# Moving one-hot matrices, weight splits and the last down product in a two-layer mixture-of-experts decoder on one core

## The chip, the cores and the metric

One core of a Trainium2 chip runs the whole program in one launch. The metric is device time in microseconds (us): the median over runs of the time of one execution. The program's engines are TensorE (PE in the profile, its weight loads PEld), VectorE (DVE), ScalarE (ACT), GpSimd (POOL) and SyncE (SP), which here issues nearly all the transfers.

## What is computed

Two layers over 256 tokens of width 1024. Each layer projects the tokens (w_in), runs three mixers (differential attention, a short gated convolution, cross attention into 256 memory tokens with its own weights w_mem_kv), merges them, adds the residual and normalises, and then does the same with a mixture of 16 experts (a gate, an up and a down matrix each), of which a token uses two, both in the one of four groups of experts that its router picks.

```
for l in range(2):
    mix = (sum_i sigmoid(G_i) * (y_i @ P_i)) @ w_out[l]
    x = layer_norm(ALPHA * x + mix, ln1_g[l], ln1_b[l])
    f = sum over the token's 2 experts e: gate_e * ((silu(x @ w_gate[l,e]) * (x @ w_up[l,e])) @ w_down[l,e])
    x = layer_norm(ALPHA * x + f, ln2_g[l], ln2_b[l])
```

## The kernel before

**Weights.** All large weights come in tiles of 1 MB, in one stream on SP's queue (`fetch`, L145), in the order of their use. A tile is asked for when its turn comes within a look-ahead (7 tiles in the mixers, 14 in the expert part, 8 near its end) and one of the 19 buffers it shares with the split weights is free. Weights of the mixers are split into a high and a low part, one half tile at a time (`pump`): ACT copies the high part (L179), DVE subtracts it to get the low part (L181). A product then takes three passes on PE: high weight by high and low activation (L217, L218), low weight by high activation (L220). Expert weights are used whole (`whole`), without a split.

**Order.** The order of PE's instructions is written out by hand: PE runs them in the order of the code. The orders of the other engines are set by a scheduler from the same code, so an edit moves rows there that it doesn't mention. Each engine runs its own list in order, and waits on semaphores.

**Start.** The first thing PE does is to transpose the memory tokens (`transposed`, L288: 16 transposes, four banks, each evicted as a high part on ACT, L206, and a low part on DVE, L207). Then come the first products with w_mem_kv: `mem_units` has four units of `ws_block`, which use halves 1 to 4, and then `mv_units` (L352), which use halves 5 to 8, first two passes with the high part of a half and then one with its low part.

**Expert part.** Eight steps p of two experts each. Each token has a slot in the list of its expert (at most 64 tokens an expert; a rare overflow is handled under an `If`, L1049, which every engine passes: it reads a count into a register and branches). For each group of four experts `places` (L885, DVE) builds a one-hot matrix pf, `gather` (L902, PE) multiplies the tokens by it and `scatter_maps` turns it (a copy pd on ACT, L912, small products on PE, L918 and L928) into the matrices that bring results back. These run one group ahead, in pieces between the projections (`steps`). A step then has the gate and up projections (`project`, L958), their product h (`gated`, L971, DVE), transposes of h (`hidden`, L980, with evictions L982 and L983), the `down` product (L993: 32 matmuls over four tiles of w_down, two tiles for each half of the inner dimension, both column halves for each), a split of its two column halves (yh on ACT, L206, yl on DVE, L207), and `combine` (L1007), which adds the results into four accumulators that stay in PSUM over all eight steps.

**End of a layer.** After the last `down` comes the `If`, then `combine` for the column halves, c = 0 and 1. `residual` adds the accumulators to x (L309, four times, on DVE) and gets the mean (L310), the variance (a square on ACT, L312) and its root (POOL, L313 and L314); `normalise` (L317, L321, DVE) applies gain and shift, loaded as gb by two transfers that POOL issues (L295, L296). In layer 0 the next layer's memory units follow on PE (their transposes are done earlier, at L288), beside the norm; then x is transposed.

Of the kernel before, what the change touches and what calls it, by code (L numbers as in the profile page):

```python
# [11 lines left out]
F32 = mybir.dt.float32  # L12
# [9 lines left out]
S = 256  # L22
DEPTH = 2
# [15 lines left out]
REV = (0, 0, 0, 1)  # L39
WARM = 20  # L40
WARM2 = 0
FILL = 20700
NU = 5
BETWEEN = 3
# [11 lines left out]
def trunk(ctx: ExitStack, tc: tile.TileContext, x, mem, positions, w_in, lq1, lk1, lq2, lk2, subln, conv_w,  # L56
# [9 lines left out]
    def bank(shape, tag="g", dtype=F32):  # L66
        return ps.tile(shape, dtype, name="ps_" + tag, tag=tag, bufs=4)
# [4 lines left out]
    def small(shape, dtype, name):  # L72
        return sb.tile(shape, dtype, name=name, tag="S", bufs=S_BUFS)
# [204 lines left out]
    cmask2 = cmask[:, None, :].to_broadcast([128, 2, 128])  # L278


    def transposed(src):

        th, tl = big([128, KD, S], F32R, "th"), big([128, KD, S], F32R, "tl")
        for k in range(0, KD, 2):
            b = bank([128, 2, S])
            for a in range(2):
                for t in range(2):
                    nc.tensor.transpose(b[:, a, t * 128:(t + 1) * 128],  # L288
                                        src[:, t, (k + a) * 128:(k + a + 1) * 128], ident)
            state["last"] = split(th[:, k:k + 2, :], tl[:, k:k + 2, :], b)  # L290
        return th, tl
# [8 lines left out]
        nc.gpsimd.tensor_scalar(v, v, EPS, None, op0=OP.add)  # L300
        nc.gpsimd.tensor_tensor(v, v, mhalf[:, 0:1], op=OP.pow)

    def residual(xt, acc, st, t):

        sm = sb.tile([128, 2], F32, name="rsum", bufs=2)
        nm, rstd = st[:, 0, t:t + 1], st[:, 1, t:t + 1]
        for c in range(2):
            v = xt[:, t, c * 512:(c + 1) * 512]
            nc.vector.scalar_tensor_tensor(v, v, ALPHA, acc[c], op0=OP.mult, op1=OP.add, accum_out=sm[:, c:c + 1])  # L309
        nc.vector.tensor_scalar(nm, sm[:, 0:1], sm[:, 1:2], -1.0 / D, op0=OP.add, op1=OP.mult)  # L310
        sq = small([128, D], BF, "sqx")
        nc.scalar.activation(sq, xt[:, t, :], AF.Square, bias=nm, accum_out=rstd)  # L312
        nc.gpsimd.tensor_scalar(rstd, rstd, 1.0 / D, EPS, op0=OP.mult, op1=OP.add)  # L313
        nc.gpsimd.tensor_tensor(rstd, rstd, mhalf[:, 0:1], op=OP.pow)  # L314
# [25 lines left out]
    def mv_units(act, dsts):  # L340
# [15 lines left out]
        for t in range(2):  # L356
            nc.scalar.activation(dsts[t], b[t], AF.Copy)

    mT = {0: transposed(mts.pop(0))}
    state["act"], state["dve"] = state["last"]  # L360
    units = mem_units(0)
# [498 lines left out]
    def warm(n):  # L860

        if n:
            b = bank([128, 4, 128])
            for _ in range(n):
                for i in range(4):
                    mm(b[:, i, :], identb, onesb, start=True, stop=True)

    def moe(l, xt, lt, st, gb):
        routing = route(l, lt, st)
        slot = next(routing)  # L870
# [10 lines left out]
        PF, XG, CT, GS = {}, {}, {}, {}  # L881

        def places(g):
            pf = small([128, 2, EG, CAP], F32R, "pf")
            ins = nc.vector.tensor_tensor(pf, i64[:, None, None, :].to_broadcast([128, 2, EG, CAP]),  # L885
                                          slot[:, :, g * EG:(g + 1) * EG, None].to_broadcast([128, 2, EG, CAP]),
                                          op=OP.is_equal)
            if g == 0:
                state["dve"] = ins
            PF[g] = pf  # L890

        def gather(g):

# [14 lines left out]

        def scatter_maps(g):

            pd = small([128, 2, 2, 2 * CAP], BF, "pd")
            nc.scalar.activation(pd, PF[g].bitcast(F32).rearrange("p t (i e) s -> p t i (e s)", i=2), AF.Copy)  # L912
            yield
            b = bank([128, 2, 2, 4])
            for i in range(2):
                for t in range(2):
# [13 lines left out]
            nc.scalar.activation(CT[g], b, AF.Copy)  # L930

        def group(g):
            places(g)
            yield from gather(g)
            yield from scatter_maps(g)
            yield

        state["ahead"] = STEADY
        prep = group(0)
        next(prep)  # L940
        gx, gp, cnti = next(routing)
# [34 lines left out]
        def hidden(h):  # L976

            b = bank([128, 4, 128])
            for f in range(4):
                nc.tensor.transpose(b[:, f, :], h[:, f, :], ident)  # L980
            hT = small([128, 4, 128], F32, "hT")
            nc.scalar.activation(hT[:, 0:2], b[:, 0:2], AF.Copy)  # L982
            nc.vector.tensor_copy(hT[:, 2:4], b[:, 2:4])  # L983
            return hT

        def down(h):
            bs = [bank([128, 512]) for _ in range(2)]
# [22 lines left out]
        def steps(n):  # L1010
            for _ in range(n):
                next(prep, None)
# [7 lines left out]
        for p in range(last + 1):  # L1020
# [19 lines left out]
            if pend is not None:  # L1040
                combine(*pend)
            steps(4)
            pend = p, down(hT[0])
            steps(4)
            if p < last:
                u = project(p + 1)
            else:
                most = nc.values_load(cnti[0:1, 0:1], min_val=0, max_val=S)
                with tc.If(most > CAP):  # L1049
                    overflow(l, xt, gx)  # L1050
        for c in range(2):
            combine(*pend, (c,))
        return xt, acc


    for l in range(DEPTH):
# [13 lines left out]
                state["act"] = scores(l, rT[1], lt, 1)  # L1070

        mixers(l, xT, done)
        xt, acc = moe(l, xt, lt, st, gb[0])
        last = l + 1 == DEPTH
        gb, st = gain_shift(ln2_g[l], ln2_b[l]), sb.tile([128, 2, 2], F32, name="lnst", bufs=2)
        for t in range(2):
            residual(xt, acc[t], st, t)
# [45 lines left out]
```

## Time and profile before

| what | value |
|---|---|
| time, median of 3 runs (least, most) | 1178.52 us (1176.53, 1179.73) |
| the profiled execution: its time, its span | 1174.73 us, 1173.0 us |
| PE busy | 1077.0 us, 92% of the span |
| DVE, ACT, POOL busy | 525.6, 421.2, 42.0 us |
| mean granted clock of TensorE | 0.970 |
| moved by DMA | 311.76 MB, mean 266 GB/s |

Times in the rows are in us from the span's start. Start and duration stand first in a row of a timeline; a stretch in brackets at its end is idle time of the engine before the row, and behind the arrow is what ended it. The profiled execution is 3.79 us faster than the median of the runs.

### The profile page before, as it was taken

The numbers are of one execution on the slowest core, as the hardware profiler recorded it, in microseconds if no ns is written. First come the engines' busy times: TensorE is split into PE (matmuls) and PEld (weight loads), VectorE is DVE, ScalarE is ACT, GpSimd is POOL, SyncE is SP. The second block draws the span as 40 slices with busy tenths as digits, with TensorE's granted clock in tenths as the row PEclk, the third lists the DMA queues.
The fourth block names the chain that finished last, engine by engine and source line by source line (L and its number), as shares of the span: only waits on it lengthen the run. The fifth ranks groups of instructions, "written<-read, shape, count | busy, mean of one in ns | idle before, by whom it ended". The sixth has DMA issues, their size and how long they took to land. (4 is left out here: it accounts for less than half of the span.)

```text
span 1173.0 us, 16717 instructions
## 1 busy us (share of the span) xinstructions
PE 1077.0 (92%) x6917; PEld 790.7 (67%) x6917; DVE 525.6 (45%) x874; ACT 421.2 (36%) x731; POOL 42.0 (4%) x87
## 2 busy tenths in 40 slices
PE   6988899999987999999989888999998889999995
PEld 6877899999974334343478878999998643344332
DVE  3968657545454111110447677565554611111114
ACT  3767645434332101010146666544433311011111
POOL 2000000000001000000010000000000110000001
PEclk9999899999988999999989899999999989999998
DMA  9925434555694999999996343356657669999993
GB/s 315 338 81 156 124 108 141 174 190 179 222 352 156 423 421 420 422 420 420 401 304 213 103 135 108 109 166 186 188 180 291 248 262 422 421 421 420 421 420 151
DMA packets 118609, 311.76 MB, mean 266 GB/s; under 512 B 5426, under 2 KB 83440, under 8 KB 93952
## 3 DMA queue, kind: packets, MB, share of 16 engines
q1 hardware_dynamic: 116192, 304.63, 70.0%
q0 software_dynamic: 1760, 5.35, 1.3%
q8 instruction: 56, 0.92, 0.3%
q10 hardware_dynamic: 576, 0.66, 0.2%
q14 instruction: 25, 0.20, 0.1%
HBM read 309.57 MB, written 1.05 MB: 265 GB/s over the span
## 5 line engine op out<-in xcount | busy, mean ns | idle before, releaser
L181 DVE TENSOR_TENSOR hl<-raw,hl 128x1024 fp32r<-128x1024 f32 x192 | 231.2, 1222 | 114.4 <-ACT hl L179 113.9
L217 PE MATMUL ps_g<-th,hl 128*128 128x256 f32 x960 | 246.6, 293 | 13.4 <-ACT hl L179 13.4
L179 ACT ACTIVATE hl<-raw 128x1024 fp32r<-128x1024 f32 x192 | 198.1, 1057 | 128.3 <-PE ps_g L220 64.9
L218 PE MATMUL ps_g<-tl,hl 128*128 128x256 f32 x960 | 242.1, 288 | 0.0
L958 PE MATMUL ps_g<-raw,xg 128*64 128x512 f32 x1024 | 229.1, 597 | 0.0
L217 PEld LDWEIGHTS ps_g<-th,hl 128*128 128x128 f32 x960 | 189.7, 198 | 18.1 <-ACT hl L179 15.9
L218 PEld LDWEIGHTS ps_g<-tl,hl 128*128 128x128 f32 x960 | 189.8, 198 | 0.1
L958 PEld LDWEIGHTS ps_g<-raw,xg 128*64 128x64 f32 x1024 | 71.5, 137 | 134.2 <-issue 131.5
L220 PE MATMUL ps_g<-th,hl 128*128 128x256 f32 x960 | 136.9, 286 | 0.7 <-DVE hl L181 0.7
L220 PEld LDWEIGHTS ps_g<-th,hl 128*128 128x128 f32 x960 | 125.8, 195 | 1.4 <-DVE hl L181 1.4
L993 PE MATMUL ps_g<-raw,hT 128*64 128x512 f32 x512 | 113.4, 595 | 0.0
L207 DVE TENSOR_TENSOR yl<-ps_g,yh 128x512 fp32r<-128x512 f32 x32 | 22.1, 690 | 149.8 <-ACT yh L206 149.8
L993 PEld LDWEIGHTS ps_g<-raw,hT 128*64 128x64 f32 x512 | 35.7, 137 | 68.0 <-issue 66.6
L206 ACT ACTIVATE yh<-ps_g 128x512 fp32r<-128x512 f32 x32 | 19.1, 597 | 116.9 <-PE ps_g L993 116.9
L971 DVE SCALAR_TENSOR_TENSOR h<-ps_g,gs,gate 128x512 f32<-128x512 f32 x16 | 17.8, 1111 | 89.3 <-PE ps_g L958 89.3
L352 PE MATMUL ps_g<-hl,th 128*128 128x512 f32 x192 | 52.9, 406 | 0.0
L982 ACT ACTIVATE hT<-ps_g 128x256 f32<-128x256 f32 x16 | 6.1, 383 | 116.7 <-PE ps_g L980 116.7
L678 PE MATMUL ps_acc<-hl,mh 128*128 128x512 f32 x128 | 37.7, 423 | 6.4 <-ACT hl L179 6.4
L902 PE MATMUL ps_g<-pf,xh 128*128 128x256 f32 x128 | 29.6, 316 | 13.2 <-DVE pf L885 13.2
L352 PEld LDWEIGHTS ps_g<-hl,th 128*128 128x128 f32 x192 | 36.0, 194 | 7.4 <-issue 0.7
L902 PEld LDWEIGHTS ps_g<-pf,xh 128*128 128x128 f32 x128 | 22.3, 212 | 25.3 <-issue 22.7
L907 ACT ACTIVATE xg<-ps_g 128x512 f32<-128x512 f32 x16 | 9.6, 597 | 76.7 <-PE ps_g L902 76.7
(236 smaller groups left out, 1276.0 us busy)
## 6 DMA issues: line engine op xcount, KB each, us to landing
raw<-in_w_in SPq DMA_DIRECT2D x64, 1024.0 KB, 5.7
raw<-in_w_exp_gate SPq DMA_DIRECT2D x64, 1024.0 KB, 14.5
raw<-in_w_exp_up SPq DMA_DIRECT2D x64, 1024.0 KB, 14.2
raw<-in_w_exp_down SPq DMA_DIRECT2D x64, 1024.0 KB, 17.0
raw<-in_w_mem_kv SPq DMA_DIRECT2D x8, 1024.0 KB, 12.4
raw<-in_w_br_attn SPq DMA_DIRECT2D x8, 1024.0 KB, 5.1
raw<-in_w_out SPq DMA_DIRECT2D x8, 1024.0 KB, 5.0
raw<-in_w_br_conv SPq DMA_DIRECT2D x8, 512.0 KB, 3.6
```

The source lines that it names most:

```text
L179: nc.scalar.activation(hi, src, AF.Copy)
L181: nc.vector.tensor_tensor(lo, src, hi.bitcast(F32), op=OP.subtract)
L206: return (nc.scalar.activation(hi, src, AF.Copy), nc.vector.tensor_tensor(lo, src, hi.bitcast(F32), op=OP.subtract))
L207: nc.vector.tensor_tensor(lo, src, hi.bitcast(F32), op=OP.subtract))
L217: mm(dst, wh[:, k0 + k, :], ah[:, k, :], start=(k == 0), stop=False)
L218: mm(dst, wh[:, k0 + k, :], al[:, k, :], start=False, stop=False)
L220: mm(dst, wl[:, k0 + k, :], ah[:, k, :], start=False, stop=(k == n - 1))
L352: mm(b[t], a[:, k, t * 128:(t + 1) * 128], ww[:, kk, :], start=(k == 0 and a is ah and ww is wh), stop=(k == KD - 1 and ww is wl))
L678: mm(acc[t][c], a[:, i, t * 128:(t + 1) * 128], ww[:, 0, c * 512:(c + 1) * 512], start=(j == 0 and s == 0), stop=(j == 3 and s == n - 1))
L902: mm(b[:, a], xs[:, t, (k + a) * 128:(k + a + 1) * 128], pf[:, t], start=(i == 0 and t == 0), stop=(i == 1 and t == 1))
L958: mm(b[both[i]], xg[:, k, c + i * CAP:c + (i + 1) * CAP], w[i][:, kk, :], start=(k == 0), stop=(k == KD - 1))
L993: mm(bs[c][both[i]], h[:, 2 * j + f, both[i]], w[i][:, f, c * 512:(c + 1) * 512], start=(j == 0 and f == 0), stop=(j == 1 and f == 1))
```

## The change

1. At the very start PE runs 56 matmuls of constant 128x128 bf16 matrices (`warm(WARM0)`, 14 times four) before the transposes of the memory tokens.
2. `places(g + 1)`, which builds pf of the next group, stands right behind the gather of group g, and makes pd too; `scatter_maps` no longer makes pd. For group 0 it stands ahead of everything.
3. The `If` of the overflow stands ahead of the last down product of a layer, no longer behind it. That product is done by column halves (`down_last`): all 4 tiles are taken at once, the column half 0 is finished over both halves of the inner dimension, then half 1 begins; ahead of the last quarter, half 0 is combined and added to x (`half`, `added`).
4. Except in the last layer, `pump(4)` splits four halves of the next layer's w_mem_kv between the last down product and the combine of column half 1. `residual` takes the sums of the half that was already added.

```diff
+WARM0 = 14
...
+    def added(xt, acc, sm, t, c):
+        v = xt[:, t, c * 512:(c + 1) * 512]
+        nc.vector.scalar_tensor_tensor(v, v, ALPHA, acc[c], op0=OP.mult, op1=OP.add, accum_out=sm[:, c:c + 1])
...
+    warm(WARM0)
     mT = {0: transposed(mts.pop(0))}
...
             PF[g] = pf
+            pd = PD[g] = small([128, 2, 2, 2 * CAP], BF, "pd")
+            nc.scalar.activation(pd, pf.bitcast(F32).rearrange("p t (i e) s -> p t i (e s)", i=2), AF.Copy)
...
         def group(g):
-            places(g)
             yield from gather(g)
+            yield
+            if g + 1 < E // EG:
+                places(g + 1)
             yield from scatter_maps(g)
             yield
...
+        def down_last(h, mid):
+
+            w = [(whole(), whole()) for _ in range(2)]
+            ys = []
+            for c in range(2):
+                b = bank([128, 512])
+                for j in range(2):
+                    if c and j:
+                        mid(ys[0])
+                    for f in range(2):
+                        for i in range(2):
+                            mm(b[both[i]], h[:, 2 * j + f, both[i]], w[j][i][:, f, c * 512:(c + 1) * 512],
+                               start=(j == 0 and f == 0), stop=(j == 1 and f == 1))
+                yh, yl = small([128, 512], F32R, "yh"), small([128, 512], F32R, "yl")
+                split(yh, yl, b)
+                ys.append((yh, yl))
+            return ys
...
             steps(4)
-            pend = p, down(hT[0])
-            steps(4)
             if p < last:
+                pend = p, down(hT[0])
+                steps(4)
                 u = project(p + 1)
-            else:
-                most = nc.values_load(cnti[0:1, 0:1], min_val=0, max_val=S)
-                with tc.If(most > CAP):
-                    overflow(l, xt, gx)
-        for c in range(2):
-            combine(*pend, (c,))
-        return xt, acc
+        most = nc.values_load(cnti[0:1, 0:1], min_val=0, max_val=S)
+        with tc.If(most > CAP):
+            overflow(l, xt, gx)
+        sums = [sb.tile([128, 2], F32, name="rsum", bufs=4) for _ in range(2)]
+
+        def half(y):
+            combine(last, [y], (0,))
+            for t in range(2):
+                added(xt, acc[t], sums[t], t, 0)
+
+        ys = down_last(hT[0], half)
+        if l + 1 < DEPTH:
+            pump(4)
+        combine(last, ys, (1,))
+        return xt, acc, sums
```

The lines of the changed kernel have moved: L885 is L891, L922 is L928, L971 is L980, L181 is L182, L207 is L208, L309 is L314, L310 is L323, L313 and L314 are L326 and L327, L317 and L321 are L330 and L334, L295 and L296 are L304 and L305, and the `If` is at L1075.

On DVE, in the expert part of layer 0, around the build of group 1's one-hot matrix. Before:

```order
288 L885 TENSOR_TENSOR pf<-i_106,slot 128x512
289 L905 COPY xg<-ps_g 128x512 x2
290 L922 TENSOR_REDUCE gs<-ps_g 64x2 x2
291 L971 SCALAR_TENSOR_TENSOR h<-ps_g,gs,gate 128x128x4
292 L885 TENSOR_TENSOR pf<-i_106,slot 128x512
293 L983 COPY hT<-ps_g 128x256
```

Now:

```order
288 L891 TENSOR_TENSOR pf<-i_106,slot 128x512
289 L913 COPY xg<-ps_g 128x512 x2
290 L891 TENSOR_TENSOR pf<-i_106,slot 128x512
291 L928 TENSOR_REDUCE gs<-ps_g 64x2 x2
292 L980 SCALAR_TENSOR_TENSOR h<-ps_g,gs,gate 128x128x4
293 L992 COPY hT<-ps_g 128x256
```

The second pf, which the gather of group 1 takes, stood behind the first h and now stands ahead of it.

On DVE, from the `If` at the end of layer 0 to the splits of w_mem_kv (hl). Before:

```order
351 L1049 UNCONDITIONAL_BRANCH
352 L309 SCALAR_TENSOR_TENSOR xt,rsum<-xt,ps_acc 128x512 x4
353 L310 TENSOR_SCALAR lnst<-rsum 128x1 x2
354 L317 SCALAR_TENSOR_TENSOR xt<-xt,lnst,gb 128x1024 x2
355 L321 SCALAR_TENSOR_TENSOR xt<-xt,lnst,gb 128x1024 x2
356 L181 TENSOR_TENSOR hl<-raw,hl 128x1024 x8
```

Now:

```order
350 L1075 UNCONDITIONAL_BRANCH
351 L208 TENSOR_TENSOR yl<-ps_g,yh 128x512
352 L314 SCALAR_TENSOR_TENSOR xt,rsum<-xt,ps_acc 128x512 x2
353 L208 TENSOR_TENSOR yl<-ps_g,yh 128x512
354 L314 SCALAR_TENSOR_TENSOR xt,rsum<-xt,ps_acc 128x512
355 L182 TENSOR_TENSOR hl<-raw,hl 128x1024 x2
356 L323 TENSOR_SCALAR lnst<-rsum 128x1
357 L314 SCALAR_TENSOR_TENSOR xt,rsum<-xt,ps_acc 128x512
358 L182 TENSOR_TENSOR hl<-raw,hl 128x1024 x2
359 L323 TENSOR_SCALAR lnst<-rsum 128x1
360 L330 SCALAR_TENSOR_TENSOR xt<-xt,lnst,gb 128x1024 x2
361 L334 SCALAR_TENSOR_TENSOR xt<-xt,lnst,gb 128x1024 x2
362 L182 TENSOR_TENSOR hl<-raw,hl 128x1024 x4
```

Of the eight low parts four now stand ahead of the norm's two passes and four still behind them.

On POOL, at the same place, the loads of gain and shift. Before:

```order
58 L1049 UNCONDITIONAL_BRANCH
59 L295 DMA gb<-in_ln_g 128x1024
60 L296 DMA gb<-in_ln_b 128x1024
61 L313 TENSOR_SCALAR lnst<-lnst 128x1
62 L314 TENSOR_TENSOR lnst<-lnst,mhalf 128x1
```

Now:

```order
58 L1075 UNCONDITIONAL_BRANCH
59 L326 TENSOR_SCALAR lnst<-lnst 128x1
60 L304 DMA gb<-in_ln_g 128x1024
61 L305 DMA gb<-in_ln_b 128x1024
62 L327 TENSOR_TENSOR lnst<-lnst,mhalf 128x1
```

The two transfers stood first behind the branch and now stand behind the first step of the variance of the first 128 tokens, for which the square on ACT must be done. At the end of layer 1 their place is the old one.

## Rows read from the trace of the kernel before

**Rows 1.** The page: busy time of the engines, and over the span in 40 slices the mean busy share of the DMA engines, in tenths.
```profile
PE 1077.0 (92%) x6917; PEld 790.7 (67%) x6917; DVE 525.6 (45%) x874; ACT 421.2 (36%) x731; POOL 42.0 (4%) x87
...
DMA  9925434555694999999996343356657669999993
```

**Rows 2.** The waits of PE, totals over the whole span: who waited for whom, us in total, times, the longest.
```profile
PE ps_g L217 <- ACT hl L179: 13.4, 5, 5.8
PE ps_g L902 <- DVE pf L885: 13.2, 8, 1.9
PE ps_g L918 <- ACT pd L912: 3.6, 6, 0.6
```

**Rows 3.** Stretches of the span: length, PE's busy time and instructions, its granted clock (1.00 is full), the busy share of the DMA engines, GB/s.
```profile
372.00:540.00 168.00, 160.67 (x796) 1.00 1.00 412
540.00:570.00 30.00, 30.00 (x138) 1.00 1.01 421
590.00:593.30 3.30, 3.14 (x14) 0.50 1.09 349
593.40:604.00 10.60, 9.88 (x83) 1.00 0.74 260
```

**Rows 4.** The timeline of PE in the expert part of layer 0: a gather that waits for pf; the last up projection; the transposes behind it.
```profile
386.46 0.47 PE L902 MATMUL ps_g<-pf,xh 128*128 128x256 f32 x2 [1.89 <-DVE pf L885]
...
562.88 7.50 PE L958 MATMUL ps_g<-raw,xg 128*64 128x512 f32 x32
570.32 1.97 PE L288 MATMUL ps_g<-ident,mt 128*128 128x128 f32 x16
```

**Rows 5.** Transfers of weights: when SP issued the last up tile and the last down tile of layer 0 and the last down tile of layer 1 (timeline), and behind each, KB and us from issue to landing (the list of transfers of that moment).
```profile
546.89 0.33 SPq L145 DMA_DIRECT2D raw<-in_w_exp_up  x1
...
raw<-in_w_exp_up SPq DMA_DIRECT2D x1, 1024.0 KB, 19.8
...
556.82 0.33 SPq L145 DMA_DIRECT2D raw<-in_w_exp_down  x1
...
raw<-in_w_exp_down SPq DMA_DIRECT2D x1, 1024.0 KB, 21.5
...
1130.51 0.33 SPq L145 DMA_DIRECT2D raw<-in_w_exp_down  x1
...
raw<-in_w_exp_down SPq DMA_DIRECT2D x1, 1024.0 KB, 23.1
```

**Rows 6.** Transfers of gain and shift that POOL issues: those issued at 341 to 342 us, at 569 to 570 us (the end of layer 0), and, the second transfer alone, at 1133 us, each with KB and us from issue to landing (lists of transfers of these moments).
```profile
gb<-in_ln_g POOLq DMA_DIRECT2D x1, 512.0 KB, 4.7
gb<-in_ln_b POOLq DMA_DIRECT2D x1, 512.0 KB, 6.0
...
gb<-in_ln_g POOLq DMA_DIRECT2D x1, 512.0 KB, 8.0
gb<-in_ln_b POOLq DMA_DIRECT2D x1, 512.0 KB, 9.7
...
gb<-in_ln_b POOLq DMA_DIRECT2D x1, 512.0 KB, 11.9
```

**Rows 7.** The start: the issue of the first tiles of w_mem_kv, the landing of the first of them (list of transfers), the transposes on PE, the first high parts on ACT, the first product; and from later in the run the 80 constant products that the router's part has (timelines).
```profile
1.65 2.02 SPq L145 DMA_DIRECT2D raw<-in_w_mem_kv  x2
...
raw<-in_w_mem_kv SPq DMA_DIRECT2D x1, 1024.0 KB, 9.7
...
8.22 3.46 PE L288 MATMUL ps_g<-ident,mt 128*128 128x128 f32 x15 [1.22 <-DMA mt<-in_mem]
...
12.22 4.13 ACT L179 ACTIVATE hl<-raw 128x1024 fp32r<-128x1024 f32 x4
...
13.32 0.58 PE L217 MATMUL ps_g<-th,hl 128*128 128x256 f32 x1 [1.63 <-ACT hl L179]
...
353.58 4.64 PE L866 MATMUL ps_g<-onesb,identb 128*128 128x128 bf16 x80
```

**Rows 8.** The timeline around the end of layer 0: last down product, residual, square, variance, high parts, first memory unit, low parts, the units from half 5 on, and the transposes of x.
```profile
574.83 7.14 PE L993 MATMUL ps_g<-raw,hT 128*64 128x512 f32 x32
...
584.04 0.69 DVE L309 SCALAR_TENSOR_TENSOR xt<-xt,ps_acc 128x512 f32<-128x512 f32 x1 [0.71 <-PE ps_acc L1007]
...
586.78 1.15 ACT L312 ACTIVATE sqx<-xt,lnst 128x1024 bf16<-128x1024 f32 x1 [4.18 <-DVE lnst L310]
...
588.12 1.14 POOL L313 TENSOR_SCALAR lnst<-lnst 128x1 f32<-128x1 f32 x1 [17.74 <-ACT sqx L312]
...
589.07 5.78 ACT L179 ACTIVATE hl<-raw 128x1024 fp32r<-128x1024 f32 x6
...
590.16 0.58 PE L217 MATMUL ps_g<-th,hl 128*128 128x256 f32 x1 [5.79 <-ACT hl L179]
...
593.16 9.17 DVE L181 TENSOR_TENSOR hl<-raw,hl 128x1024 fp32r<-128x1024 f32 x8
...
604.11 1.09 PE L352 MATMUL ps_g<-hl,th 128*128 128x512 f32 x4
...
615.03 1.91 PE L288 MATMUL ps_g<-ident,xt 128*128 128x128 f32 x16
```

**Rows 9.** The timeline around the end of layer 1: last down product, mean.
```profile
1151.77 7.09 PE L993 MATMUL ps_g<-raw,hT 128*64 128x512 f32 x32
...
1162.89 0.33 DVE L310 TENSOR_SCALAR lnst<-rsum 128x1 f32<-128x1 f32 x2
```

More of the change, by code (lines that the diff above doesn't have):

```diff
@@ L278, in trunk, with warm @@
     cmask2 = cmask[:, None, :].to_broadcast([128, 2, 128])
+    def warm(n):
+        if n:
+            b = bank([128, 4, 128])
+            for _ in range(n):
+                for i in range(4):
+                    mm(b[:, i, :], identb, onesb, start=True, stop=True)
     def transposed(src):
@@ L301, in rsqrt, with residual @@
         nc.gpsimd.tensor_tensor(v, v, mhalf[:, 0:1], op=OP.pow)
-    def residual(xt, acc, st, t):
-        sm = sb.tile([128, 2], F32, name="rsum", bufs=2)
+    def added(xt, acc, sm, t, c):
+        v = xt[:, t, c * 512:(c + 1) * 512]
+        nc.vector.scalar_tensor_tensor(v, v, ALPHA, acc[c], op0=OP.mult, op1=OP.add, accum_out=sm[:, c:c + 1])
+    def residual(xt, acc, st, t, sm=None):
         nm, rstd = st[:, 0, t:t + 1], st[:, 1, t:t + 1]
-        for c in range(2):
-            v = xt[:, t, c * 512:(c + 1) * 512]
-            nc.vector.scalar_tensor_tensor(v, v, ALPHA, acc[c], op0=OP.mult, op1=OP.add, accum_out=sm[:, c:c + 1])
+        if sm is None:
+            sm = sb.tile([128, 2], F32, name="rsum", bufs=4)
+            added(xt, acc, sm, t, 0)
+        added(xt, acc, sm, t, 1)
         nc.vector.tensor_scalar(nm, sm[:, 0:1], sm[:, 1:2], -1.0 / D, op0=OP.add, op1=OP.mult)
@@ L858, in overflow @@
                     nc.vector.scalar_tensor_tensor(v, b[t], gx[:, t, ds(e, 1)], v, op0=OP.mult, op1=OP.add)
[L860 to L866, printed above, removed]
     def moe(l, xt, lt, st, gb):
@@ L880, in moe @@
             nc.vector.tensor_tensor(turned(xl, t), xt[:, t, :], turned(xh, t).bitcast(F32), op=OP.subtract)
-        PF, XG, CT, GS = {}, {}, {}, {}
+        PF, PD, XG, CT, GS = {}, {}, {}, {}, {}
         def places(g):
@@ L909, in scatter_maps @@
         def scatter_maps(g):
-            pd = small([128, 2, 2, 2 * CAP], BF, "pd")
-            nc.scalar.activation(pd, PF[g].bitcast(F32).rearrange("p t (i e) s -> p t i (e s)", i=2), AF.Copy)
-            yield
+            pd = PD[g]
             b = bank([128, 2, 2, 4])
@@ L938, in moe @@
         state["ahead"] = STEADY
+        places(0)
         prep = group(0)
@@ L1042, in moe @@
             steps(4)
-            pend = p, down(hT[0])
-            steps(4)
             if p < last:
+                pend = p, down(hT[0])
+                steps(4)
                 u = project(p + 1)
-            else:
-                most = nc.values_load(cnti[0:1, 0:1], min_val=0, max_val=S)
-                with tc.If(most > CAP):
-                    overflow(l, xt, gx)
-        for c in range(2):
-            combine(*pend, (c,))
-        return xt, acc
+        most = nc.values_load(cnti[0:1, 0:1], min_val=0, max_val=S)
[11 more added lines that the diff above has]
+        return xt, acc, sums
     for l in range(DEPTH):
@@ L1072, in trunk @@
         mixers(l, xT, done)
-        xt, acc = moe(l, xt, lt, st, gb[0])
+        xt, acc, sums = moe(l, xt, lt, st, gb[0])
         last = l + 1 == DEPTH
@@ L1076, in trunk @@
         for t in range(2):
-            residual(xt, acc[t], st, t)
+            residual(xt, acc[t], st, t, sums[t])
         src, xt = xt, big([128, 2, D], F32, "xt")
```

## The prediction

> **What bounds the kernel now.** I read the page first. PE is busy for 92% of the span, DVE and ACT for less than half, so PE seems to be the bound; but in the second line the DMA engines stand at 9 tenths or more in two long stretches, and these are the expert parts [rows 1]. So there are two kinds of stages, and a gain has to be read in each by itself. The waits of PE come next [rows 2]: three of them belong to what is changed, the gather's wait for the one-hot matrix pf (13.2 us in 8), the scatter products' wait for its copy pd (3.6 in 6), and the wait of a memory unit for its first high part (13.4 in 5, of which 5.8 in one). Then I cut the expert part of layer 0 into stretches [rows 3]: from 372 to 570 us the DMA share is 1.00 to 1.01 at 412 to 421 GB/s, while PE has idle time only before 540 (168.0 less 160.67 is 7.3 us). The reader is to see that PE's idle time there lies in a stage whose end the weights set. The last up tile is issued at 546.89 and lands 19.8 us later, at 566.7; the projection that needs it ran from 562.88 and took 7.50 us, so its second half, which begins about 3.7 us in, found its tile just landed [rows 4, 5]. The last down tile lands at 556.82 + 21.5 = 578.3, and the second half of the last down product begins at 574.83 + 3.57 = 578.4 [rows 5, 8]. Work taken from PE before this point returns as a wait for these tiles. In the rest of the program PE is the bound, and the four places below are read there. The profiled execution (1174.73 us) is 3.8 us under the median; I take the sum as a difference against its trace and put it on the median. Differences under 0.3% (3.5 us) can't be told from none.
>
> **The start (part 1).** 80 such constant products took 4.64 us, 0.058 each [rows 7]. The 15 transposes of the start take 3.46 us, 0.23 each, and the same ones later 1.97 us for 16, 0.12 each [rows 4, 7]: PE starts at half speed. At half speed the 56 new products take at most 56 x 0.116 = 6.5 us, and PE idles until 8.22 anyway, so they cost nothing as long as they begin before 1.7 us; their operands are made by two short DVE steps, and without that cover each us of delay is a us lost. What they bring: at full speed the transposes end at 8.22 + 15 x 0.12 = 10.1, not 11.7. The first high part then is bound by its tile, issued at 1.65, landing 9.7 us later at 11.35, not 12.22 [rows 7]. So the first unit moves up by 0.9 us. If the clock also stays at full through that unit, whose matmuls before cost 0.1 us each too much for some 14 of them (by the stretch at clock 0.50: 14 in 3.14 us, against 83 in 9.88 at 1.00 [rows 3]), another 1.4 is won. PE idles from 10.1 to 12.4 in between, which is longer than the 1.89 us that left the clock at 1.00 [rows 3, 4] and shorter than the 5.79 us behind which it stood at 0.50 [rows 3, 8]. Ends: 0 and 2.3; I take 1.2, the 0.9 and a bit of the rest.
>
> **The one-hot matrices (part 2).** Six of the gathers' waits, at up to 1.89 us, and the 3.6 us for pd go away: 6 x 1.87 + 3.6 = 14.8 us of PE time, half of it in each layer [rows 2, 4]. DVE and ACT do the same work earlier, on engines with over half their time free [rows 1]. In layer 0 I cost it at nothing, since the last tiles land when they did. In layer 1 the last down tile lands at 1130.51 + 23.1 = 1153.6, and the down product began at 1151.77, second half at 1155.3 [rows 5, 9]: 1.7 us of room, which bounds that gain.
>
> **The last down by column halves (part 3).** The new order needs the last tile behind the first quarter (7.09 / 4 = 1.8 us) instead of the second. In layer 1 that is 1151.77 + 1.8 = 1153.6, the very time it lands: the 1.7 us of room are used up, and nothing of part 2 arrives. After it, 5.3 us of matmuls and the combine of column half 0 in the middle (four matmuls of 512 columns, 1.0 us by the L352 row [rows 8]) put the end of the product about 1.0 us later; two of the four residual steps (0.6 each, from 584.04 to 586.5 with the next row of the mean [rows 8]) then leave the tail, 1.2 us; the branch in front of the product, which each engine passes, costs 0.2 to 0.5 (0.71 us of DVE's idle in front of L309 contains it now [rows 8]). Sum between -0.5 and +0.6; I take 0.
>
> **The boundary of the layers (parts 3 and 4).** In layer 0 the tile lands earlier: gain and shift (1.05 MB, 2.5 us at 421 GB/s [rows 3, 6]) no longer run beside it, since POOL issues them later, so it is there by 575.8, before 574.83 + 1.8. The down product ends at 574.83 + 0.5 (branch) + 7.14 + 1.0 = 583.5. ACT splits column half 1 (0.6), then makes the first high part (5.78 / 6 = 0.96): unit 1 can start at about 585.4 instead of 590.16, 4.7 us earlier, without the 5.79 us of idle and the half clock behind it (1.5 us more) [rows 3, 8]. Whether this arrives is decided at half 5. Units 1 to 4 take 24 x 0.12 = 2.9 us each, to 597.0; the first two passes of half 5 are 1.85 us more, and at 598.9 PE needs its low part. On DVE that stands behind the four passes of the norm, which need gb, and gb is now issued behind the first variance step on POOL. Four high parts (3.8 us from 584.1) and the square (1.15) come ahead of that on ACT, and two low parts ahead of the mean on DVE, so POOL issues at about 590.5, in place of 569. The loads took 4.7 and 6.0 us with little else moving, 8.0 and 9.7 beside the weights [rows 6]: g lands at 595.2 to 598.5. Four passes at 1.15 (the L181 row, of the same width [rows 8]) and one low part are 5.8 us: half 5 is complete at 601.0 to 604.3, a PE wait of 2.1 to 5.4 us. From there 615.03 - 604.11 - 1.85 = 9.1 us remain to the transposes: 610.1 to 613.4, plus 1.5 if the clock falls in this wait, so 610.1 to 614.9, against 615.03. Ends: 4.9 and 0.1; what decides is whether the weight stream is active at 591, and the share there was 1.09 before [rows 3], so I take a value below the middle, 2.0. SP passes its branch ahead of four loads of w_in now; these are first needed behind 615 and the share from 593 to 604 is only 0.74 [rows 3], so I cost that at nothing; without this cover each us of delay would be one of PE.
>
> **Sum.** 1.2 + 0 + 0 + 2.0 = 3.2 us less: 1178.5 - 3.2 = 1175.3.
>
> **A rule against the rows.** The rows of gb at the end of layer 0 show 8.0 and 9.7 us beside the weight stream [rows 6]. The Trainium skill ("DMA: Bandwidth & Descriptors", Queues, rings and completion order) says that a DMA engine takes turns between the queues it has work for, a packet each; by that rule gb, on a queue of its own, would be held up little, and the boundary would be near its better end, 4.9 us instead of 2.0. The two times in a full stream, nearly twice the 4.7 and 6.0 of the light one, speak against it.
>
> **The rivals.**
> - Gain and shift land quickly. The mechanism is the light load of the rows, 4.7 us: half 5 complete at 601.0, a wait of 2.1 us, near the 1.89 that kept the clock. For it: SP is held up by its own branch at that time. Time: 1178.5 - 1.2 - 4.9 = 1172.4.
> - They land as late as beside a full stream, 8 us and more. The boundary then gives nothing, or takes up to 2 us with the fallen clock; with the start it is 1177.5 to 1180. For it: the share of 1.09 at 590 to 593.
> - Slower: one mechanism, the gb load behind the square, on DVE's list ahead of half 5. Its point is g landing at 598.5 + 0.1, about 8 us after the issue: from there each us of landing is a us of the program. At the 11.9 us that the load of layer 1 took [rows 6] half 5 is complete at 608.2, and 9.1 + 1.5 us later it is 618.8, 3.8 us slower there: 1178.5 + 3.8 - 0.9 = 1181.4. At 20 us, which a tile of the stream takes [rows 5], it would be 1190. Against it: at 569 the same loads took 8.0 and 9.7 in a full stream.
> - PE is the bound of the expert part after all, and part 2 arrives: up to 14.8 us more, 1160.5, or half of it where one layer alone follows, 1167.9. Against it is the share of 1.00 with the tiles' landing; for it, PE's 92%.
> - The start does nothing, because the clock falls again in the 2.3 us of idle: 0.9 or 0 instead of 1.2. This is within the forecast's own range.
>
> **How the numbers follow.** Forecast (1 to 5 us less) 0.42, quick gb 0.18, PE-bound 0.06, late gb without a loss over 3.5 us 0.22, slower by more 0.12. Faster by over 0.3% are the quick gb, the PE-bound case and nearly half of the forecast (it reaches past 3.5 us): 0.44; within, the rest of the forecast and the late gb: 0.44; slower 0.12. The range reaches from 1168.5, which leaves out most of the PE-bound case, to 1181.0, which leaves out the slower one: about 0.17 outside.
>
> **What would show it.** Right: no waits of L902 for pf but the two first ones, yet the expert stretch of layer 0 as long, with new idle time of PE for transfers at its end; unit 1 of the boundary at 585 to 586, and a new wait of L352 for DVE's low part (L182), with gb issued at 590 to 591; the first unit of the program at about 12.4. Wrong: the expert stretch shorter by several us, a gb that lands within 5 us and no wait of L352, or transposes of x later than before.

## The result and the profile after

The change made the kernel slower. Six runs of each kernel gave a median of 1184.35 us (1182.32 to 1186.02) against 1178.22 us (1173.16 to 1179.73): a ratio of 1.0065, 95% interval 1.0048 to 1.0081, some 6 to 8 us. The profiled execution took 1186.02 us with a span of 1184.3 us, 11.3 more than the one of before; of this gap, 5 us are only that before's profiled execution (1174.73 us) lay 3.5 us under the median of its six runs and this one 1.7 over its own. One execution of the experiments, 5989.29 us in the run of the changed kernel without constant products, is left out of its ratio.

The page after: busy time, and the DMA engines' share in 40 slices, beside [rows 1].

```profile
PE 1091.2 (92%) x6973; PEld 798.1 (67%) x6973; DVE 526.5 (44%) x874; ACT 421.9 (36%) x731; POOL 40.3 (3%) x87
...
DMA  9925434555685999999994343355558669999991
```

The waits of PE, beside [rows 2]: who waited for whom, us in total, times, the longest.

```profile
PE ps_g L218 <- ACT hl L180: 8.4, 4, 2.4
...
PE ps_g L365 <- DVE hl L182: 4.8, 1, 4.8
PE ps_g L967 <- DMA raw<-in_w_exp_up: 4.5, 4, 1.7
PE ps_g L1006 <- PEq L1075: 3.4, 2, 3.0
...
PE ps_g L1006 <- issue: 2.2, 1, 2.2
...
PE ps_g L910 <- DVE pf L891: 2.1, 2, 1.1
```

The wait for pf went from 13.2 to 2.1 us, that for the first high part lost its 5.8 us piece, and the one for pd is gone. New waits stand in their place. The gate and up projections (L967) waited for nothing before; now they wait for 9.6 us in all, 4.5 of them for up tiles. Three more decide what follows: for the low part of half 5 (L365), and twice in the last down product (L1006), behind the branch (L1075) and for "issue", that is, for nothing that the profile shows.

To see where the time went, I cut both traces at events that don't depend on the order of the code: the first gather of a layer, the landing of its last down tile (issue plus time to landing), the transposes of x, and the end. In us, from the timelines and transfer lists of one execution each:

| stretch | before | after |
|---|---|---|
| start to first gather, layer 0 | 364.5 | 365.9 |
| to the last down tile's landing, layer 0 | 213.8 | 212.8 |
| to the transposes of x | 36.7 | 43.6 |
| to the first gather, layer 1 | 325.8 | 324.4 |
| to the last down tile's landing, layer 1 | 212.7 | 212.5 |
| to the end | 19.4 | 25.1 |

The expert parts hardly changed (1.0 and 0.2 us shorter), while the ends of the two layers lost 6.9 and 5.7 us. The timeline of PE, DVE and POOL at the end of layer 0, beside [rows 8]:

```profile
577.26 1.94 PE L1006 MATMUL ps_g<-raw,hT 128*64 128x512 f32 x8 [0.41 <-PEq L1075]
581.42 5.35 PE L1006 MATMUL ps_g<-raw,hT 128*64 128x512 f32 x16 [2.21 <-issue]
...
592.02 0.28 PE L218 MATMUL ps_g<-th,hl 128*128 128x256 f32 x1
...
596.95 0.58 POOL L304 DMA_DIRECT2D gb<-in_ln_g  x1 [0.31 <-DMA raw<-in_w_in]
...
604.28 2.48 DVE L330 SCALAR_TENSOR_TENSOR xt<-xt,lnst,gb 128x1024 f32<-128x1024 f32 x2 [6.44 <-DMA gb<-in_ln_g]
...
610.35 3.78 PE L365 MATMUL ps_g<-hl,th 128*128 128x512 f32 x8 [4.82 <-DVE hl L182]
...
622.27 1.91 PE L297 MATMUL ps_g<-ident,xt 128*128 128x128 f32 x16
```

And of layer 1, beside [rows 9], where the last tile had landed at 1159.2:

```profile
1156.31 0.39 PE L1034 MATMUL ps_acc<-yl,ct 128*128 128x512 f32 x1
1159.68 8.33 PE L1006 MATMUL ps_g<-raw,hT 128*64 128x512 f32 x24 [2.99 <-PEq L1075]
...
1174.19 0.33 DVE L323 TENSOR_SCALAR lnst<-rsum 128x1 f32<-128x1 f32 x2
```

24 of these matmuls take 5.3 us by [rows 9], here 8.33. The granted clock says why (1.00 is full). Stretches: length, PE's busy time and instructions, clock, DMA share, GB/s.

```profile
582.00:587.00 5.00, 5.00 (x17) 0.66 1.06 375
...
612.00:620.00 8.00, 8.00 (x28) 0.74 1.09 353
...
1160.00:1166.00 6.00, 6.00 (x16) 0.53 0.00 0
```

So each of the last three waits is paid twice, once as a wait and once at about half speed behind it. What PE waited for at L1075 shows in the instructions of that line (duration in ns: least, median, most; first and last start):

```profile
L1075 PEldq COMPARE_BRANCH  x2: 352/2460/4567, 575.0 to 1154.7; - x2
L1075 ACTq COMPARE_BRANCH  x2: 45/45/45, 575.6 to 1155.2; - x2
```

PE's branch took 0.35 us in layer 0 and 4.57 in layer 1, where ACT's took 0.05. And the list of transfers from 1154 to 1162 us shows two on the queue of instructions, 16 KB each (packets, MB, share of the engines):

```profile
q8 instruction: 2, 0.03, 1.6%
```

Over a run this queue moves 57 such blocks, about one for each 250 instructions that PE executes (6973 matmuls and as many weight loads). The idea that the experiments had to test: PE fetches its code in blocks of 16 KB, the branch leaps over the code of the overflow, and where the code behind that leap is in a block not yet there, PE stands until it has come. Whether the weights that fill the DMA engines at that time lengthen the stall is not shown: the block's own transfer took 1.1 us there, and 0.9 to 1.4 us anywhere in the trace of before. Before the change the branch was passed while 4 us of matmuls were still queued on PE (it took 0.35 us at 1154.87 in the trace of before, and the product ran to 1158.86).

### The profile page after: what moved, and what is told of

It is laid out like the page before. It is cut to its first block, busy times and chain, and to the rows that moved or that the text cites. A ratio compares the mean times of both kernels' runs of the same rounds, so it can differ in the third digit from the quotient of the medians.

```text
span 1184.3 us, 16817 instructions
## 1 busy us (share of the span) xinstructions
PE 1091.2 (92%) x6973; PEld 798.1 (67%) x6973; DVE 526.5 (44%) x874; ACT 421.9 (36%) x731; POOL 40.3 (3%) x87
## 3 DMA queue, kind: packets, MB, share of 16 engines
q0 software_dynamic: 1760, 5.35, 1.2%
## 5 line engine op out<-in xcount | busy, mean ns | idle before, releaser
L182 DVE TENSOR_TENSOR hl<-raw,hl 128x1024 fp32r<-128x1024 f32 x192 | 231.5, 1222 | 116.6 <-ACT hl L180 115.4
L967 PE MATMUL ps_g<-raw,xg 128*64 128x512 f32 x1024 | 232.5, 596 | 9.6 <-DMA raw<-in_w_exp_up 4.5
L218 PEld LDWEIGHTS ps_g<-th,hl 128*128 128x128 f32 x960 | 189.0, 197 | 12.5 <-ACT hl L180 10.3
L967 PEld LDWEIGHTS ps_g<-raw,xg 128*64 128x64 f32 x1024 | 73.2, 137 | 145.5 <-issue 125.0
L1020 PE MATMUL ps_g<-raw,hT 128*64 128x512 f32 x448 | 101.2, 596 | 0.9 <-DMA raw<-in_w_exp_down 0.9
L208 DVE TENSOR_TENSOR yl<-ps_g,yh 128x512 fp32r<-128x512 f32 x32 | 22.1, 690 | 162.3 <-ACT yh L207 162.3
L1020 PEld LDWEIGHTS ps_g<-raw,hT 128*64 128x64 f32 x448 | 31.3, 137 | 61.9 <-issue 58.6
L207 ACT ACTIVATE yh<-ps_g 128x512 fp32r<-128x512 f32 x32 | 19.2, 599 | 133.5 <-PE ps_g L1020 104.5
L365 PE MATMUL ps_g<-hl,th 128*128 128x512 f32 x192 | 55.8, 423 | 4.8 <-DVE hl L182 4.8
L980 DVE SCALAR_TENSOR_TENSOR h<-ps_g,gs,gate 128x512 f32<-128x512 f32 x16 | 18.1, 1131 | 93.1 <-PE ps_g L967 93.1
L365 PEld LDWEIGHTS ps_g<-hl,th 128*128 128x128 f32 x192 | 38.0, 205 | 13.4 <-DVE hl L182 5.2
L546 ACT ACTIVATE p<-ps_acc,sm 128x128 f32<-128x128 f32 x64 | 26.2, 425 | 23.5 <-DVE sm L541 23.5
L692 PEld LDWEIGHTS ps_acc<-hl,mh 128*128 128x128 f32 x128 | 25.1, 201 | 12.4 <-ACT hl L180 6.8
L992 DVE COPY hT<-ps_g 128x256 f32<-128x256 f32 x16 | 6.8, 425 | 59.2 <-ACT hT L991 59.2
## 6 DMA issues: line engine op xcount, KB each, us to landing
raw<-in_w_mem_kv SPq DMA_DIRECT2D x8, 1024.0 KB, 12.5
```

The source lines that it names most:

```text
L182: nc.vector.tensor_tensor(lo, src, hi.bitcast(F32), op=OP.subtract)
L207: return (nc.scalar.activation(hi, src, AF.Copy), nc.vector.tensor_tensor(lo, src, hi.bitcast(F32), op=OP.subtract))
L208: nc.vector.tensor_tensor(lo, src, hi.bitcast(F32), op=OP.subtract))
L218: mm(dst, wh[:, k0 + k, :], ah[:, k, :], start=(k == 0), stop=False)
L365: mm(b[t], a[:, k, t * 128:(t + 1) * 128], ww[:, kk, :], start=(k == 0 and a is ah and ww is wh), stop=(k == KD - 1 and ww is wl))
L546: nc.scalar.activation(e[:, sl], bs[c][:, sl], AF.Exp, scale=0.125, bias=st[:, 0, c, qb:qb + 1], accum_out=st[:, 1, c, qb:qb + 1])
```

## Experiments

The first four take parts alone, or move the branch. A ratio is the time over that of before; behind it stands its 95% interval.

**Part 1 alone.** The start of the change (`warm` and `WARM0`) in the kernel before.

```diff
+WARM0 = 14
...
+    warm(WARM0)
     mT = {0: transposed(mts.pop(0))}
```

> The kernel before with part 1 alone, the 56 constant products ahead of the first transposes. Theory A (the start's gain is real and is given back by the clock): first unit at 12.4 to 12.6 us at full speed, 2.2 us ahead of before at 30 us, and by 90 us the lead is gone, with spells of granted clock 0.7 to 0.8 in the mixers of layer 0 where before shows 1.00; time within 3 us of before. Rival B (the lead stays, and it was another part that lost it): the lead of 2.2 us still stands at 300 us, time 2 us less than before.

Measured: 1.0009 (0.9987 to 1.0030). The first product began at 12.75, but at a low clock, so there was no lead of 2.2 us; at 30 us it was 0.45.

```profile
12.50:17.00 4.50, 4.25 (x23) 0.62 1.06 352
```

The low clock in the mixers came as expected, but not through the start: the run with the branch alone, below, whose start is that of before, had it too (0.79 from 52 to 60 us, 0.72 from 70 to 76, 0.76 from 83 to 90). Before's profiled execution had 1.00 there. The first of these stretches, before and then with the branch alone:

```profile
52.00:60.00 8.00, 6.48 (x34) 1.00 0.65 210
...
52.00:60.00 8.00, 6.48 (x29) 0.79 0.66 214
```

PE's instructions up to there are the same in both, so these spells differ between executions of equal code. In the changed kernel's trace, with spells at the same places, PE goes from 2.2 us ahead of before at 52 us to 2.4 behind it at 87 us. A result I had not expected: in layer 0 PE's branch took 3.16 us.

```profile
L1051 PEldq COMPARE_BRANCH  x2: 335/1748/3162, 582.2 to 1158.4; - x2
```

Nothing was changed there but the number of PE's instructions in front of it, by 112. Here 3.9 us of matmuls were still queued on PE when it branched (the product ran from 578.97 to 586.06), and PE felt 0.19 us of the stall.

**Part 2 alone.** The one-hot matrices and pd made behind the gather, in the kernel before.

```diff
...
         def group(g):
-            places(g)
             yield from gather(g)
+            yield
+            if g + 1 < E // EG:
+                places(g + 1)
...
```

> The kernel before with part 2 alone, one-hot matrices made right behind the gather. Theory A (weights set the end of the expert parts): PE leads before by some 5 us at 510 us, then waits for the last up tiles, and the last up projection of layer 0 stands where it did, within 0.5 us; in layer 1 at most 1.7 us less; time 0 to 2 us less than before. Rival B (PE sets the end): 7 us less in each layer, 14 in all.

Measured: 1.0010 (0.9984 to 1.0036). Theory A, in each of its steps: at 510 us PE was 6.8 us ahead of before; then it met the tiles.

```profile
561.42 3.65 PE L961 MATMUL ps_g<-raw,xg 128*64 128x512 f32 x16 [1.32 <-DMA raw<-in_w_exp_up]
566.38 3.65 PE L961 MATMUL ps_g<-raw,xg 128*64 128x512 f32 x14 [1.31 <-DMA raw<-in_w_exp_up]
```

The last 14 matmuls of the last up projection, which wait for its second tile, began at 566.38, where they had begun at 566.75. From the first gather to the last landing it is 212.7 us in layer 1, as before.

**The branch alone.** Only the branch is moved ahead of the last down product, in the kernel before.

```diff
+            if p == last:
+                most = nc.values_load(cnti[0:1, 0:1], min_val=0, max_val=S)
+                with tc.If(most > CAP):
+                    overflow(l, xt, gx)
             pend = p, down(hT[0])
...
```

> The kernel before with one step of part 3 alone: the branch of the overflow ahead of the last down product, which keeps its old order (both column halves for each half of the inner dimension). Theory A (behind the branch PE must get its next instructions while the weight stream fills the DMA engines, and stands for 2 to 4 us in front of or early in the product, which then runs at half the clock): 3 to 9 us more than before in all, with idle time of PE of 2 us or more between the branch and the eighth matmul of the product in both layers. Rival B (a branch costs what I took for it, 0.2 to 0.5 us each): 0.5 to 1 us more.

Measured: 1.0013 (0.9987 to 1.0039). Theory A failed as I had put it: the branch cost what the prediction had said, 0.4 us in each layer.

```profile
1152.25 7.09 PE L993 MATMUL ps_g<-raw,hT 128*64 128x512 f32 x32 [0.41 <-PEq L1045]
```

In both layers it is 0.35 us on PE, and a wait of 0.41. So a branch ahead of the product isn't bad in itself. With the 3.16 us of part 1 alone, the number of instructions in front of it came under suspicion.

**The branch in the middle.** The changed kernel with the branch behind column half 0.

```diff
...
                 ys.append((yh, yl))
+                if c == 0:
+                    branch()
...
```

> The changed kernel with the branch moved to the middle of the last down product, behind column half 0 and its split, so that 16 matmuls of PE are still to come when it branches (the order on POOL then has the loads of gain and shift ahead of the variance again, as before). Theory A (branch and late gb cost the time): no idle time of PE over 1 us at the branch in layer 1, no wait of half 5 for its low part in layer 0, 6 to 10 us less than the changed kernel, so 4 us less than before up to the same. Rival B (the order by column halves costs the time, since it needs the last tile sooner): as the changed kernel, 4 to 8 us more than before.

Measured: 1.0018 (0.9997 to 1.0039), between the two. The stall did not go: the branch took 6.52 us in layer 0 and 3.37 in layer 1, of which PE felt 5.54 and 2.19. Of the 16 matmuls ahead of it only 1.3 and 1.5 us were left when PE branched, less than either stall.

```profile
PE ps_g L1006 <- PEq L1080: 7.7, 2, 5.5
```

But it had gb early, by the order on POOL, and no wait of L365. The stretch to the transposes of x was 38.5 us, that to the end 22.3.

The next four test the place of the branch in its block, and the load of gain and shift.

**No constant products**, and **a whole block of them**: the changed kernel with 0, and with 128 (256 instructions; one execution).

```diff
-WARM0 = 14
+WARM0 = 0
```

> The changed kernel without its 56 constant products (no part 1). Theory A (PE's code comes in pages of 16 KB; the 112 added instructions move the branch of the overflow within a page, so that the code behind it has to be fetched while PE stands): no PE stall at the branch in either layer, as in the run with the branch alone moved ahead, whose branch stands at the same place; from the last landing of a down tile to the end 19 to 20 us instead of 25.1, from the landing in layer 0 to the transposes of x 38 to 41 us instead of 43.6; time 1 to 4 us over before, 3 to 6 us under the changed kernel. Rival B (the wait at the branch belongs to the order by column halves, which needs all four tiles): the stall of 3 to 5 us in layer 1 stays, time as the changed kernel.

```diff
-WARM0 = 14
+WARM0 = 32
```

> The changed kernel with 128 constant products at the start instead of 56, that is 256 instructions of PE, one whole page, instead of 112. Theory A (the place within a page decides): no PE stall at the branch, as with none of them, though more instructions are added; the branch takes 0.3 to 0.4 us on PE in both layers. Rival B (more code in front, more stall, whatever the page): stalls of 2 us and more in both layers.

Measured: 0.9989 (0.9972 to 1.0006) without them, and one execution at 1173.13 us with 128, before's median being 1176.56. Without them 1 to 4 us over before had been expected. The branch on PE, without them and then with 128:

```profile
L1075 PEldq COMPARE_BRANCH  x2: 353/356/358, 570.3 to 1144.3; - x2
```

```profile
L1075 PEldq COMPARE_BRANCH  x2: 323/338/353, 574.0 to 1147.0; - x2
```

With 0 and 256 added instructions there is no stall; with 112 there are stalls of 2.2 and 3.0 us. That tells a place within a block from the mere length of the code, and from the column halves, which all three have. Without the products the list of transfers has one block of code around the branch of layer 1 (1143 to 1151 us) instead of two:

```profile
q8 instruction: 1, 0.02, 0.9%
```

The traces show it closer, over all twelve profiled kernels of this document. There are seven stalls, five at a branch and two of 2.2 us ("issue") eight matmuls behind one. In each, one block of 16 KB is on its way, and PE goes on, or its branch ends, 1.3 to 1.7 us after that transfer has ended. The place can be counted too, in PE's instructions in front of the branch, from the kernel without constant products. Where the branch stands up to 61 of them later (seven kernels), or 255, there is no stall in either layer; at 111 and at 152 there is one in both; at some 162, part 1 alone, there is one in layer 0 and none in layer 1. The borders of the blocks themselves are not in the trace.

The stretch to the transposes is 38.8 and 38.3 us instead of 43.6, that to the end 19.9 in both instead of 25.1. 4.8 and 5.2 us (the first from the run with none) make 10.0 us for the 56 products; by the two ratios it is 1.0065 less 0.9989, 9 us.

**Gain and shift early**, first in the changed kernel, then also without constant products.

```diff
+        gb2 = gain_shift(ln2_g[l], ln2_b[l])
         most = nc.values_load(cnti[0:1, 0:1], min_val=0, max_val=S)
...
-        gb, st = gain_shift(ln2_g[l], ln2_b[l]), sb.tile([128, 2, 2], F32, name="lnst", bufs=2)
+        st = sb.tile([128, 2, 2], F32, name="lnst", bufs=2)
```

> The changed kernel with the loads of gain and shift issued by POOL ahead of the branch at the end of both layers, as before the change. Theory A (the late load is one of two losses): DVE's low part of half 5 is in time, the wait of PE of 4.8 us for it and the half clock behind it go, the stretch from the last landing in layer 0 to the transposes of x is 4 to 6 us shorter than the changed kernel's 43.6, while the last down tile of layer 0 lands 2 us later; the stall at the branch stays. Time 2 to 4 us under the changed kernel. Rival B (gb is hidden anyway): no change of that stretch, time as the changed kernel.

Measured: 0.9996 (0.9972 to 1.0020), some 8 us less than the changed kernel, where 2 to 4 had been expected. The stretch to the transposes is 32.7 us instead of 43.6, also more than expected; in layer 1 the stall stays.

```profile
1150.25 8.18 PE L1006 MATMUL ps_g<-raw,hT 128*64 128x512 f32 x24 [3.30 <-PEq L1076]
```

> The changed kernel with both repairs: no constant products (the branch at its old place in a page) and gain and shift loaded ahead of the branch. Theory A (these two are the whole loss): from the last landing in layer 0 to the transposes of x 31 to 35 us (36.7 before), to the end in layer 1 19 to 20 us; time 2 to 5 us under before. Rival B (something else of the change costs as much): no better than before.

Measured: 0.9949 (0.9930 to 0.9968), median 1171.31 us: faster than before. The stretches are 31.4 us (36.7 before) and 19.9 (19.4 before); the last tile of layer 0 lands 215.2 us behind the first gather instead of 212.8, since gb is in the stream again. That is theory A; the time, 5 to 6 us under before, is a little beyond its 2 to 5. DVE has gb when it comes to it, and half 5 doesn't wait:

```profile
594.94 2.48 DVE L330 SCALAR_TENSOR_TENSOR xt<-xt,lnst,gb 128x1024 f32<-128x1024 f32 x2
...
600.71 1.11 PE L365 MATMUL ps_g<-hl,th 128*128 128x512 f32 x4
601.66 1.08 PE L365 MATMUL ps_g<-hl,tl 128*128 128x512 f32 x4
602.58 1.99 PE L365 MATMUL ps_g<-hl,th 128*128 128x512 f32 x8
```

The last two start from this one.

**A start of few instructions.** 12 products of 512 columns.

```diff
+WARM0 = 12
...
-    warm(WARM0)
+    b = bank([128, 4, 128])
+    for _ in range(WARM0):
+        mm(b, identb, onesb[:, None, :].to_broadcast([128, 4, 128]), start=True, stop=True)
```

> The doubly repaired kernel (gain and shift ahead of the branch) with the start given back in another form: 12 constant products of 512 columns, 24 instructions of PE instead of 112. Theory A (the start itself is harmless and its 112 instructions did the harm through the code page): no PE stall over 1 us at the branch in either layer, the first unit at 12.4 to 12.8 us; time as the doubly repaired kernel without a start or up to 2 us less, 0.4 to 0.7% under before. Rival B (24 instructions already reach the place within the page where the code behind the branch is missing): a stall of 2 us and more at a branch, 3 to 6 us more than without a start.

Measured: 0.9946 (0.9921 to 0.9970), median 1169.72 us. No stall at the branch:

```profile
L1078 PEldq COMPARE_BRANCH  x2: 352/355/358, 573.4 to 1141.8; - x2
```

The first product began at 12.70, against 13.39 without a start, but at a clock of 0.62 from 12.5 to 17.0. Against the kernel without a start the two intervals don't tell a gain.

**The old tail in layer 1.** The last layer alone gets `down` and the branch in their old order.

```diff
+        if l + 1 == DEPTH:
+            gb2 = gain_shift(ln2_g[l], ln2_b[l])
+            pend = last, down(hT[0])
...
+            for c in range(2):
+                combine(*pend, (c,))
+            return xt, acc, (None, None), gb2
```

> The doubly repaired kernel without a start, in which the last layer alone has its last down product and its branch in the old order, so that column halves and the branch ahead are kept in layer 0 alone. Theory A (in layer 1 the order by column halves loses about what it wins, as I put it, -0.5 to +0.6): from the last landing to the end 19 to 19.5 us instead of 19.9, time within 1 us of the doubly repaired kernel. Rival B (the column halves pay in layer 1): 21 us and more, time 1.5 us or more over it.

Measured: 0.9948 (0.9927 to 0.9968), the same. The stretch from the last landing to the end is 18.6 us, 1.3 less than with column halves; but the last tile landed 1.1 us later behind the first gather of the layer (213.3 and 212.2 us), so that from this gather to the end it is 231.9 and 232.1 us. In layer 1 the column halves neither win nor lose.

## Why the prediction was wrong

The forecast was 3.2 us less; measured were some 6 us more, outside the range.

**The step that failed** is that of the start: "they cost nothing as long as they begin before 1.7 us". They began at 1.67, and PE's time was indeed free there.

```profile
1.67 4.94 PE L288 MATMUL ps_g<-onesb,identb 128*128 128x128 bf16 x56 [1.67 <-DVE identb L269]
...
8.22 1.86 PE L297 MATMUL ps_g<-ident,mt 128*128 128x128 f32 x15 [1.49 <-DMA mt<-in_mem]
12.48 0.39 PE L218 MATMUL ps_g<-th,hl 128*128 128x256 f32 x1 [2.41 <-ACT hl L180]
```

The transposes ended at 10.1 and the first product began at 12.5, as worked out. But I counted the instructions as time and not as code. 112 more instructions moved the branch over the overflow's code to a place from which the code behind it isn't at hand, 570 and 1150 us later; with the half speed behind the stalls that is about 9 us, as much as the whole miss: without them the kernel took 0.9989 of before's time, inside the range. (Where gb is early too they are worth less: 0.9996 less 0.9949, 5.5 us, by the stretches 1.3 us in layer 0 and 5.3 in layer 1.) The step that the branch in front of the product costs 0.2 to 0.5 is right by itself (0.41 measured, where no block is missing) and wrong in this kernel for the same reason: too little is left in PE's queue to hide a fetch. The Trainium skill ("Runtime: NRT & Kernel Launch", Instruction fetch mechanics) has the rule, that code comes in blocks of 16 KB, 256 instructions, and that a taken branch to a block not at hand forces a fetch before PE goes on. The runs agree: one transfer of 16 KB for some 250 instructions, and 256 more instructions leave the branch at 0.35 us. The prediction did not weigh it; the trace of before, where a branch on PE takes 0.35 us in both layers, gave no sign of it.

**The boundary.** The mechanism was right: gb is issued behind the square, and half 5 is late. It shows best without the constant products, where no stall of the branch comes in between.

```profile
PE ps_g L365 <- DVE hl L182: 5.2, 1, 5.2
```

There gb was issued 14.1 us behind the landing of the last down tile (588.09 and 573.95), where the prediction had 14.7, and from that landing to the transposes it took 38.8 us, where the prediction's chain gives 34.3 to 39.1 (610.1 to 614.9, less 575.8). The terms were mis-sized. The wait of 5.2 us is near the end of my 2.1 to 5.4, and the half clock behind it cost 1.9 us (10.92 us from the end of the wait to the transposes, 9.07 for the same matmuls in before), where I took 1.5 at most. And the last down tile, which I had 2.5 us earlier, came 0.7 us earlier behind the first gather (213.1 and 213.8), 1.0 in the changed kernel. So the boundary lost 1.4 us, tile included, where I took a gain of 2.0. (My terms for the start of unit 1 make 585.0 and not 585.4; nothing hangs on that.)

In the changed kernel unit 1 followed the combine without a wait (592.0; it was late by the branch's stall, not by the splits), the wait of L365 was 4.82 us, and the half clock behind it cost 2.9 us (11.92 against 9.07). gb was issued at 597 and not 590.5, late by the stall too.

```profile
gb<-in_ln_g POOLq DMA_DIRECT2D x1, 512.0 KB, 7.3
```

It landed 7.3 us later, near the loaded row of [rows 6], 8.0, and far from the light one, 4.7; so the trace does not bear out what the prediction drew from the Trainium skill ("DMA: Bandwidth & Descriptors", Queues, rings and completion order), that a queue of its own would hold gb up little. With gb early the stretch to the transposes was 31.4 us, a gain of 5.3 against before, of which 1.4 go back to the stream (215.2 against 213.8 to the last landing).

**What held.** Part 2 gave nothing, the tiles landing at 212.2 to 213.3 us behind the first gather of layer 1 in each kernel of which I cut the trace this way. The column halves in layer 1 gave nothing either. Four signs of being right came: the first product at 12.5, of the waits for pf only two left, new waits of PE for tiles, and the wait of L365 (L352 in before). The sign of being wrong came as well, in the transposes of x. The lead of the start, 2.2 us at 16 us, was there in the profiled execution; but in the run without constant products PE led before by 1.3 us at 18 us, since its first unit ran at full speed too, and in the run with part 1 alone the clock fell within the first unit. No time shows a gain from a start.

**The numbers.** The chance of "slower" was 0.12, and its one mechanism did not decide: it asked that g land over 8 us after its issue, but g took 7.3, and without the constant products, where it took 7.7, the kernel was not slower than before. What made it slower stood in no rival. What I should have asked of an addition that fills an idle engine is what else it uses: here, the engine's instruction stream.

## What to carry to other kernels

An instruction added where an engine is idle costs no time there, but it moves all the code behind it; near a runtime branch this can decide whether the code behind the leap is at hand, so look at the duration of the branch itself on each engine, and keep a few us of queued work on the engine when it branches (3.9 us hid all but 0.2 of a stall of 3.2 here, 1.3 us hid 1.0 of one of 6.5), or add fewer, longer instructions. A part that makes PE faster in a stage whose DMA share is 1.00 should be judged by when the last tile lands, not by the waits it removes. And where a scheduler sets the order of an engine, small loads have to be issued ahead of the work that might delay their issuer: gb's place in POOL's list was worth some 5 us without the constant products and 8 with them.

## What the runs showed of the hardware

PE's branch took 0.32 to 0.36 us in 19 of the 24 passes of these traces, and 3.2 to 6.5 us in the other five, ACT's 0.05 in every one. The block of code that PE waited for took 0.9 to 1.3 us to move.

Granted clock after a wait is not a function of the wait alone: after the same 2.2 us stall behind the branch in layer 0, the 16 matmuls behind it took 5.35 us in the changed kernel and 3.65 with gb early:

```profile
579.86 3.65 PE L1006 MATMUL ps_g<-raw,hT 128*64 128x512 f32 x16 [2.22 <-issue]
```

Spells of low clock in the mixers of layer 0 came and went between executions of the same instructions, and moved PE's place in the program by some 4.5 us; before's own runs spread from 1167.65 to 1183.02 us over 31 runs on one chip. A single profile against a single profile would have put this difference down to the change.
